# Rotary embedding of attention heads 1 to 3: from GpSimd to VectorE

## The chip, the core and the metric

The kernel runs on one core of a Trainium2 chip. The metric is the device time of one execution in microseconds. Engines are named as in the profile: PE is TensorE (PEld its weight loads), DVE is VectorE, ACT is ScalarE, POOL is GpSimd, SP is SyncE.

## What is computed

One step of a diffusion backbone with one layer: a modulated norm, an input projection, differential attention with four heads beside a depthwise convolution of 31 taps, gates, an output projection, and a gated MLP. There are 1024 latent tokens and 128 context tokens. The change touches the rotary embedding of queries and keys of the latent tokens:

```python
def apply_rope(x, cos, sin):
    shp = x.shape
    xr = x.reshape(shp[:-1] + (2, 2, QK_DIM // 4))
    x1 = xr[..., 0, :]
    x2 = xr[..., 1, :]
    c = cos[None, :, None, None].astype(x.dtype)
    s = sin[None, :, None, None].astype(x.dtype)
    out = jnp.stack([x1 * c - x2 * s, x1 * s + x2 * c], axis=-2)
    return out.reshape(shp)
...
    if rope is not None:
        q = apply_rope(q, rope[0], rope[1])
        k = apply_rope(k, rope[0], rope[1])
```

All arithmetic is fp32. A matmul is made of three, with each operand split into a high and a low part.

## The kernel before

Activations lie with channels on the 128 partitions and the 1152 tokens along the free axis, in three chunks of 384. The program has a first phase that makes the normalised input and the first projections, a second with the attention, and a third with the merge, the output projection and the MLP. The change is in the second.

**Attention and its fillers.** `attn_head` goes over the query tiles of one head, eight of latent tokens and one of context. For each tile and each of the two score maps TensorE makes scores in PSUM (tile `S`, L786 and L787), VectorE takes their minimum (`mx`, L793), ScalarE the exponential (`e`, L795), and VectorE combines the two maps (L803, L804 and the long one, L806, in this document "the combine"). TensorE transposes the combined tile (`T`, L819), ScalarE and VectorE split it into a high part (`ath`, L822) and a low one (`atl`, L823), and TensorE multiplies by the values (`O`, L834). Between these steps stand matmuls of the input projections that are not needed yet, the fillers (L242, PSUM tile `f`), in the order of `FILL_SEQ`: the queries and keys of heads 1 to 3, convolution inputs `ua2`, `ub2`, `ua3`, `ub3`, and gates.

**The rope.** When a filler has made the queries or keys of a head (`xs`, 128x1152), `proj_unit` puts off eight steps of `rope_stages`, one for each of the next ticks: a shuffle on VectorE into `sw` (L550), four multiplications by tables (L558, on `sw`, `xs`, `sw`, `xs`, 128x1024 each), an add (L562), a split in which ScalarE casts the high part `rh` (L566) and the low part is subtracted in place (L567, 128x1152), and the store to DRAM by DMAs on ScalarE's queue. The engine of the six instructions L558 (four), L562 and L567 is chosen by `op_eng`. Ropes are named by head: q0, k0 are made ahead of the attention, and q1, k1, q2, k2, q3, k3 during the attention of heads 0 to 2.

**The convolution in the background.** `conv_jobs` makes each of 31 taps in two parts: 967 columns on VectorE (L651; the first tap is L648, a multiplication alone), and 200 columns as a product on ScalarE (`tap`, L658) that GpSimd adds (L664). The tiles of a head draw them from a list, at a pace set by `PACE`. GpSimd also makes the low halves of the weights (`wlo`, L187), whose high halves ScalarE casts (L180).

**What sets the order.** The program is handed to a scheduler that plans the instructions of each engine by a cost model and priorities (scores, minima, combines and transposes of the attention have a high one); each engine then runs its instructions in the planned order. `pin` limits how far the plan may move an instruction on VectorE, TensorE and SP. So a change of engine also changes the plan around it.

Of the kernel before, what the change touches and what calls it, by code (L numbers as in the profile page):

```python
# [109 lines left out]
class Kernel:  # L110
# [419 lines left out]
    def rope_stages(self, name, xs, sw_t, hi_t):  # L530

        nc = self.nc
        h = int(name[1:])
        isq = name[0] == "q"
        cst = self.cst
        lat = xs[:, NCTX:T]
        lat3 = lat.rearrange("p (r c) -> p r c", c=GRID_W)
        box = {}

        def row(c0):  # L540
            return cst[:, c0:c0 + 16].rearrange("p (r o) -> p r o", o=1).to_broadcast([128, 16, GRID_W])

        def col(c0):
            return cst[:, c0:c0 + 64].rearrange("p (o c) -> p o c", o=1).to_broadcast([128, 16, GRID_W])

        def s0():
            if not isq:
                nc.scalar.dma_start(out=self.A["nk"][h], in_=xs[:, 0:NCTX])
            box["sw"] = sw_t()
            nc.vector.stream_shuffle(box["sw"][:, 0:NLAT], lat, [(i + 16) % 32 for i in range(32)])  # L550

        def op_eng(i):
            return nc.vector if h == 0 else nc.gpsimd

        def mul(i, tab):
            def f():
                v = lat3 if i % 2 else box["sw"][:, 0:NLAT].rearrange("p (r c) -> p r c", c=GRID_W)
                op_eng(i).tensor_tensor(out=v, in0=v, in1=tab, op=ALU.mult)  # L558
            return f

        def add():
            op_eng(4).tensor_tensor(out=lat, in0=lat, in1=box["sw"][:, 0:NLAT], op=ALU.add)  # L562

        def split():
            hi = box["hi"] = hi_t()
            nc.scalar.copy(hi.bitcast(F32R), xs)  # L566
            op_eng(5).tensor_tensor(out=xs.bitcast(F32R), in0=xs, in1=hi, op=ALU.subtract)  # L567

        def store():
            hi = box["hi"]  # L570
            if isq:
                d = self.A["qscr"][h]
                for src, r0, c, o in ((hi, 0, 0, 0), (xs, 0, 0, 64), (xs, 64, 1, 0), (hi, 64, 1, 64)):
                    nc.scalar.dma_start(out=d[o:o + 64, c, :], in_=src[r0:r0 + 64, :])
            else:
                d = self.A["kscr"][h]
                for c in range(2):
                    for o in (0, 64):
                        nc.scalar.dma_start(out=d[o:o + 64, c, 0:T], in_=hi[64 * c:64 * c + 64, :])
                nc.scalar.dma_start(out=d[:, 2, 0:T], in_=xs)  # L580
            self.stored.add(name)

        return [s0, mul(0, row(C_SA)), mul(1, row(C_CA)), mul(2, col(C_SB)), mul(3, col(C_CB)),
                add, split, store]
# [1335 lines left out]
```

## Time and profile before

| | us |
|---|---|
| median of 3 runs (1790.53 to 1791.32) | 1790.59 |
| the profiled execution | 1790.29 |
| its span, from the first to the last instruction | 1788.3 |
| TensorE busy | 1682.3 |
| VectorE busy | 1177.2 |
| GpSimd busy | 713.3 |

Busy time is that of the whole span; a stretch is read by itself, by asking for the busy time of each engine between two times. In a row of instructions the name left of the arrow is what is written, those on the right are what is read; idle time before an instruction stands in brackets with the one that ended it. Waits are put down to the instruction that came last.

### The profile page before, as it was taken

How to read it: one execution, taken by the hardware profiler on the slowest of the kernel's cores; microseconds unless marked ns; L12 is line 12 of the kernel's file. 1: busy time of each engine (PE TensorE's matmuls, PEld its weight loads, DVE VectorE, ACT ScalarE, POOL GpSimd, SP SyncE). 2: the span in 40 equal slices, each digit the busy share in tenths (PEclk: the TensorE clock that was granted, in tenths of full speed). 3: DMA queues.
4: the chain of work that ended last, by engine and by line, in shares of the span. 5: the costliest groups of instructions: out<-in, count | busy, mean ns of one | idle time of the engine just before them, and what ended most of it. 6: DMA issues, size and time to landing. Idle time of an engine off the chain costs nothing.

```text
span 1788.3 us, 25510 instructions
## 1 busy us (share of the span) xinstructions
PE 1682.3 (94%) x9928; PEld 1644.2 (92%) x9928; DVE 1177.2 (66%) x1594; ACT 751.1 (42%) x1166; POOL 713.3 (40%) x507
## 2 busy tenths in 40 slices
PE   5999989989989999889989899999999999999997
PEld 3889989978989999888989899999999999999997
DVE  5859995699697663587588765766567565333335
ACT  4424444445454554311225744545455456111111
POOL 2545782585673431544243321222222137433311
PEclk8999999999999999999999999999999999999999
DMA  8264323323325433666753364756666567622102
GB/s 312 88 190 137 103 79 104 132 69 118 120 76 182 142 105 114 235 221 205 268 174 106 85 173 114 182 131 162 150 151 150 139 148 224 175 89 101 62 12 106
DMA packets 111087, 251.96 MB, mean 141 GB/s; under 512 B 10964, under 2 KB 61816, under 8 KB 108920
## 3 DMA queue, kind: packets, MB, share of 16 engines
q1 hardware_dynamic: 45264, 120.15, 19.7%
q10 hardware_dynamic: 51592, 79.08, 13.9%
q0 software_dynamic: 14112, 51.12, 13.4%
q8 instruction: 78, 1.28, 0.3%
q14 instruction: 41, 0.34, 0.1%
HBM read 161.55 MB, written 57.30 MB: 122 GB/s over the span
## 4 chain that ended last, share of the span: by engine, by line
PE 52%; DVE 18%; DMA 8%; issue 8%; POOL 5%; ACT 3%; ACTq 1%; POOLq 0%; DVEq 0%; SPq 0%
PE f L242 15%; PE T L242 7%; DVE conv L651 7%; PE S L1499 6%; PE f L1499 6%; PE T L1499 6%; PE O L242 3%; PE O L1499 3%; DVE mx L793 2%; DMA tg<-scr_gscr 2%; PE O L834 2%; DVE e L806 2%; POOL wlo L187 1%; DVE S L1206 1%; DMA hx<-in_ada 1%
## 5 line engine op out<-in xcount | busy, mean ns | idle before, releaser
L187 POOL TENSOR_TENSOR wlo<-raw,whi 128x1024 fp32r<-128x1024 f32 x104 | 270.2, 2599 | 389.0 <-ACT whi L180 370.8
L242 PE MATMUL f<-h1h,whi 128*128 128x384 f32 x680 | 233.4, 345 | 3.9 <-ACT gt L614 3.2
L242 PE MATMUL f<-h1l,whi 128*128 128x384 f32 x680 | 234.5, 345 | 0.0
L180 ACT CAST whi<-raw 128x1024 fp32r<-128x1024 f32 x126 | 132.0, 1048 | 243.7 <-DMA raw<-in_wst 59.4
L242 PE MATMUL f<-h1h,wlo 128*128 128x384 f32 x680 | 232.0, 342 | 0.0
L1491 DVE SCALAR_TENSOR_TENSOR X<-X,vec,X 128x1153 f32<-128x1153 f32 x88 | 139.7, 1593 | 91.6 <-ACT X L1489 91.0
L651 DVE SCALAR_TENSOR_TENSOR conv<-glu,vec,conv 128x967 f32<-128x967 f32 x120 | 199.2, 1660 | 1.1
L664 POOL TENSOR_TENSOR conv<-conv,tap 128x200 f32<-128x200 f32 x120 | 115.5, 962 | 68.3 <-ACT tap L658 65.8
L242 PEld LDWEIGHTS f<-h1h,whi 128*128 128x128 f32 x680 | 130.2, 192 | 5.3 <-ACT gt L614 3.9
L242 PEld LDWEIGHTS f<-h1l,whi 128*128 128x128 f32 x680 | 130.7, 192 | 0.4
L242 PEld LDWEIGHTS f<-h1h,wlo 128*128 128x128 f32 x680 | 130.2, 192 | 0.2
L795 ACT ACTIVATE e<-S,mx 128x1152 f32<-128x1152 f32 (+1 forms) x72 | 81.2, 1128 | 70.2 <-DVE mx L793 58.7
L793 DVE TENSOR_REDUCE mx<-S 128x1 f32<-128x1152 f32 (+1 forms) x72 | 88.6, 1231 | 31.5 <-PE S L787 31.5
L658 ACT ACTIVATE tap<-glu,vec 128x200 f32<-128x200 f32 x120 | 55.5, 462 | 105.6 <-POOL conv L664 89.9
L242 PE MATMUL T<-ff,whi 128*128 128x384 f32 x360 | 92.1, 335 | 1.5 <-ACT hx L1691 1.5
L184 POOL DMA_DIRECT2D wlo<-rawx x40 | 34.4, 860 | 141.6 <-ACT wlo L183 122.9
L242 PE MATMUL f<-ff,whi 128*128 128x384 f32 x340 | 87.0, 335 | 0.5 <-ACT hx L1691 0.5
L786 PE MATMUL S<-K,q 128*128 128x384 f32 (+1 forms) x200 | 69.0, 345 | 13.3 <-ACT e L795 13.3
L823 DVE TENSOR_TENSOR atl<-T,ath 128x512 fp32r<-128x512 f32 (+1 forms) x100 | 52.0, 538 | 30.3 <-ACT ath L822 29.8
L1251 DVE SCALAR_TENSOR_TENSOR hx<-f,g,hx 128x128 f32<-128x128 f32 (+1 forms) x64 | 31.6, 515 | 58.8 <-PE f L242 58.8
L180 ACT CAST whi<-rawx 128x1024 fp32r<-128x1024 f32 x42 | 44.0, 1047 | 62.0 <-PE S L1499 23.7
L1251 DVE SCALAR_TENSOR_TENSOR hx<-T,g,hx 128x256 f32<-128x256 f32 (+1 forms) x66 | 32.3, 511 | 54.7 <-PE T L242 54.3
(438 smaller groups left out, 4961.6 us busy)
## 6 DMA issues: line engine op xcount, KB each, us to landing
raw<-in_wst SPq DMA_DIRECT2D x105, 512.0 KB, 4.2
wlo<-rawx POOLq DMA_DIRECT2D x40, 512.0 KB, 6.0
X<-scr_fscr POOLq DMA_DIRECT2D x20, 576.0 KB, 5.0
scr_fscr<-X SPq DMA_DIRECT2D x22, 512.0 KB, 5.3
wlo<-raw POOLq DMA_DIRECT2D x20, 512.0 KB, 4.8
scr_gscr<-gate ACTq DMA_DIRECT2D x48, 192.0 KB, 2.0
tg<-scr_gscr SPq DMA_DIRECT2D x24, 384.0 KB, 4.2
ada<-in_ada SPq DMA_DIRECT2D x8, 1024.0 KB, 9.9
```

The costliest lines, as they stand in the source:

```text
L180: nc.scalar.copy(hi, raw)
L187: eng.tensor_tensor(out=lo, in0=raw, in1=hi.bitcast(F32), op=ALU.subtract)
L242: nc.tensor.matmul(out, lhsT=a, rhs=b, start=(i == 0), stop=(i == n - 1))
L651: t = nc.vector.scalar_tensor_tensor(out=o, in0=glu[:, j:j + CSPLIT], scalar=w[:, j:j + 1], in1=o, op0=ALU.mult, op1=ALU.add)
L658: nc.scalar.activation(out=p, in_=glu[:, CSPLIT + j:CONVW + j], func=AF.Copy, scale=w[:, j:j + 1])
L664: t = nc.gpsimd.tensor_tensor(out=o, in0=o, in1=p, op=ALU.add)
L786: nc.tensor.matmul(S[:, j, :cw], lhsT=qt[:, c, o:o + 128], rhs=self.K[:, c, ks], start=True, stop=False)
L793: nc.vector.tensor_reduce(out=mx[:, 1:2], in_=src, axis=AX.XY, op=ALU.min)
L795: nc.scalar.activation(out=e[:, :w].rearrange("p (a b) -> p a b", a=nk), in_=src, func=AF.Exp, scale=-1.0, bias=mx[:, 1:2], accum_out=self ...
L1251: nc.vector.scalar_tensor_tensor(out=d, in0=ps[:, o:o + ln], scalar=gate[:, j, c:c + 1], in1=d, op0=ALU.mult, op1=ALU.add)
L1491: nc.vector.scalar_tensor_tensor(out=y[:, :L], in0=u[:, t:t + L], scalar=w[:, t:t + 1], in1=y[:, :L], op0=ALU.mult, op1=ALU.add)
L1499: nc.tensor.matmul(ps[:, :CH], lhsT=a[:, ws], rhs=b[:, k], start=first and k == 0 and i == 0, stop=last and k == 3 and i == 2)
```

## The change

The function that picks the engine for the six rope instructions returns VectorE for every head.

```diff
--- before.py
+++ after.py
@@ -550,7 +550,7 @@
             nc.vector.stream_shuffle(box["sw"][:, 0:NLAT], lat, [(i + 16) % 32 for i in range(32)])
 
         def op_eng(i):
-            return nc.vector if h == 0 else nc.gpsimd
+            return nc.vector
 
         def mul(i, tab):
             def f():
```

The plan moves with it. On VectorE, at q1's rope in the attention of head 0, the order before was (`os_590` is the table of the maps' sums):

```order
L550 STREAM_SHUFFLE sw<-xs 128x1024
L651 SCALAR_TENSOR_TENSOR conv<-glu,vec,conv 128x967
L823 TENSOR_TENSOR atl<-T,ath 128x4x128 x2
L651 SCALAR_TENSOR_TENSOR conv<-glu,vec,conv 128x967
L793 TENSOR_REDUCE mx<-S 128x1
L651 SCALAR_TENSOR_TENSOR conv<-glu,vec,conv 128x967 x2
L803 RECIPROCAL mx<-mx 128x1
L823 TENSOR_TENSOR atl<-T,ath 128x128
L804 TENSOR_SCALAR mx<-mx,os_590,lam 128x1
L806 SCALAR_TENSOR_TENSOR e<-e,mx 128x1152
```

and now, from the same shuffle on:

```order
L550 STREAM_SHUFFLE sw<-xs 128x1024
L651 SCALAR_TENSOR_TENSOR conv<-glu,vec,conv 128x967
L823 TENSOR_TENSOR atl<-T,ath 128x4x128
L558 TENSOR_TENSOR sw<-sw,cst 128x1024
L823 TENSOR_TENSOR atl<-T,ath 128x4x128
L558 TENSOR_TENSOR xs<-xs,cst 128x1024
L651 SCALAR_TENSOR_TENSOR conv<-glu,vec,conv 128x967
L558 TENSOR_TENSOR sw<-sw,cst 128x1024
L793 TENSOR_REDUCE mx<-S 128x1
L558 TENSOR_TENSOR xs<-xs,cst 128x1024
L823 TENSOR_TENSOR atl<-T,ath 128x128
L651 SCALAR_TENSOR_TENSOR conv<-glu,vec,conv 128x967
```

The four multiplications and the add stand between taps, minima and splits of the transposed tile; the split (L567) and the combine (L806) follow 6 and 7 rows further on, one after the other.

On GpSimd the same place read, from the last tap add ahead of the rope:

```order
L664 TENSOR_TENSOR conv<-conv,tap 128x200
L558 TENSOR_TENSOR sw<-sw,cst 128x1024
L558 TENSOR_TENSOR xs<-xs,cst 128x1024
L664 TENSOR_TENSOR conv<-conv,tap 128x200
L558 TENSOR_TENSOR sw<-sw,cst 128x1024
L558 TENSOR_TENSOR xs<-xs,cst 128x1024
L664 TENSOR_TENSOR conv<-conv,tap 128x200
L562 TENSOR_TENSOR xs<-xs,sw 128x1024
L187 TENSOR_TENSOR wlo<-raw,whi 128x1024
L664 TENSOR_TENSOR conv<-conv,tap 128x200
L567 TENSOR_TENSOR xs<-xs,rh 128x1152
```

and now:

```order
L664 TENSOR_TENSOR conv<-conv,tap 128x200 x8
L187 TENSOR_TENSOR wlo<-raw,whi 128x1024
L664 TENSOR_TENSOR conv<-conv,tap 128x200 x8
L187 TENSOR_TENSOR wlo<-raw,whi 128x1024
L664 TENSOR_TENSOR conv<-conv,tap 128x200 x7
L187 TENSOR_TENSOR wlo<-raw,whi 128x1024
L631 MEMSET glu 128x15 x3
L187 TENSOR_TENSOR wlo<-raw,whi 128x1024 x4
L917 TENSOR_TENSOR ors<-oms,cols 128x9
```

The six rope instructions are gone, and tap adds and weight halves follow one another.

On VectorE at the first tile of head 1, with q2's rope, the order before was:

```order
L550 STREAM_SHUFFLE sw<-xs 128x1024
L793 TENSOR_REDUCE mx<-S 128x1
L803 RECIPROCAL mx<-mx 128x1
L804 TENSOR_SCALAR mx<-mx,os_590,lam 128x1
L806 SCALAR_TENSOR_TENSOR e<-e,mx 128x1152
L793 TENSOR_REDUCE mx<-S 128x1
L648 TENSOR_SCALAR conv<-glu,vec 128x967
L823 TENSOR_TENSOR atl<-T,ath 128x4x128 x2
L651 SCALAR_TENSOR_TENSOR conv<-glu,vec,conv 128x967
```

and now:

```order
L550 STREAM_SHUFFLE sw<-xs 128x1024
L558 TENSOR_TENSOR sw<-sw,cst 128x1024
L793 TENSOR_REDUCE mx<-S 128x1
L558 TENSOR_TENSOR xs<-xs,cst 128x1024
L558 TENSOR_TENSOR sw<-sw,cst 128x1024
L558 TENSOR_TENSOR xs<-xs,cst 128x1024
L803 RECIPROCAL mx<-mx 128x1
L793 TENSOR_REDUCE mx<-S 128x1
L648 TENSOR_SCALAR conv<-glu,vec 128x967
L562 TENSOR_TENSOR xs<-xs,sw 128x1024
L804 TENSOR_SCALAR mx<-mx,os_590,lam 128x1
L806 SCALAR_TENSOR_TENSOR e<-e,mx 128x1152
```

Three multiplications, a second minimum, the first tap and the add stand between the first minimum and the combine, which came right behind it.

## Rows read from the trace of the kernel before

**Rows 1.** the page: busy us, share of the span and instructions of each engine.
```profile
PE 1682.3 (94%) x9928; PEld 1644.2 (92%) x9928; DVE 1177.2 (66%) x1594; ACT 751.1 (42%) x1166; POOL 713.3 (40%) x507
```

**Rows 2.** busy time by stretch; columns: stretch, us, engines (instructions), clock, DMA share, GB/s.
```profile
206.00:264.00 58.00, 51.99 (x293) 49.54 (x294) 55.80 (x52) 27.85 (x57) 46.57 (x29) 0.94 0.28 78
264.00:337.00 73.00, 71.21 (x455) 70.26 (x454) 34.51 (x54) 31.58 (x64) 19.75 (x14) 1.00 0.39 125
337.00:441.00 104.00, 95.15 (x571) 90.15 (x569) 99.14 (x96) 52.33 (x104) 79.63 (x50) 0.98 0.30 86
...
470.00:552.00 82.00, 72.72 (x436) 68.95 (x435) 79.52 (x75) 42.05 (x83) 65.06 (x39) 0.98 0.34 96
```

**Rows 3.** the chain of waits from 206 to 552 us, its shares by line.
```profile
by line: DVE conv L651 26.7%; PE f L242 18.0%; DVE mx L793 9.3%; DVE e L806 8.9%; DVE atl L823 5.3%; PE O L834 4.1%; issue 2.7%; POOL conv L664 2.6%; PE T L819 2.3%; PE S L786 2.1%; PE S L787 2.1%; ACT e L795 2.0%; DVE sw L550 1.6%; DVE mx 
```

**Rows 4.** one line: durations in ns min/median/max, first and last start us, forms.
```profile
L558 POOL TENSOR_TENSOR xs<-xs,cst x12: 1900/2880/3132, 221.4 to 527.1; 128x1024 f32<-128x1024 f32 x12
...
L558 DVE TENSOR_TENSOR xs<-xs,cst x2: 1206/1208/1211, 87.0 to 93.7; 128x1024 f32<-128x1024 f32 x2
...
L562 POOL TENSOR_TENSOR xs<-xs,sw x6: 2354/2390/3302, 233.0 to 531.6; 128x1024 f32<-128x1024 f32 x6
...
L567 POOL TENSOR_TENSOR xs<-xs,rh x6: 2655/2902/3576, 240.0 to 535.9; 128x1152 fp32r<-128x1152 f32 x6
...
L567 DVE TENSOR_TENSOR xs<-xs,e x1: 1362/1362/1362, 99.6 to 99.6; 128x1152 fp32r<-128x1152 f32 x1
...
L651 DVE SCALAR_TENSOR_TENSOR conv<-glu,vec,conv x120: 1208/1385/3457, 123.1 to 564.6; 128x967 f32<-128x967 f32 x120
```

**Rows 5.** the time line of VectorE, GpSimd and TensorE at k2's rope.
```profile
398.59 3.51 DVE L806 SCALAR_TENSOR_TENSOR e<-e,mx 128x1152 f32<-128x1152 f32 x1
...
398.53 2.35 POOL L562 TENSOR_TENSOR xs<-xs,sw 128x1024 f32<-128x1024 f32 x1
...
402.15 0.47 PE L819 MATMUL T<-cst,e 128*128 128x128 f32 x1 [2.90 <-DVE e L806]
```

**Rows 6.** busy time in the five rope windows (q1, q2, k2, q3, k3).
```profile
218.60:242.70 24.10, 20.48 (x117) 19.55 (x116) 23.29 (x18) 8.00 (x14) 24.07 (x11) 0.93 0.32 94
...
383.60:406.00 22.40, 18.85 (x112) 17.93 (x111) 22.29 (x17) 9.47 (x19) 22.40 (x12) 0.92 0.21 60
...
518.10:538.60 20.50, 17.98 (x102) 16.84 (x101) 20.43 (x14) 8.79 (x17) 20.02 (x11) 0.92 0.23 72
sum 110.30, PE 97.17 PEld 91.82 DVE 107.24 ACT 48.34 POOL 109.22; mean PE 19.43 PEld 18.36 DVE 21.45 ACT 9.67 POOL 21.84
```

**Rows 7.** the same for five windows with taps and without a rope.
```profile
sum 97.00, PE 88.07 PEld 83.37 DVE 93.09 ACT 57.84 POOL 53.81; mean PE 17.61 PEld 16.67 DVE 18.62 ACT 11.57 POOL 10.76
```

**Rows 8.** the taps on VectorE (L651) alone, in the five rope windows.
```profile
218.60:242.70 24.10, 16.41 (x8) 0.93 0.32 94
...
sum 110.30, DVE 61.18; mean DVE 12.24
```

**Rows 9.** the taps (L651) alone, in the five windows without a rope.
```profile
sum 97.00, DVE 50.39; mean DVE 10.08
```

**Rows 10.** combines (L806): seven in the rope windows, then seven in the others.
```profile
sum 110.30, DVE 17.24; mean DVE 3.45
...
sum 97.00, DVE 10.94; mean DVE 2.19
```

**Rows 11.** busy time in the window of k1's rope.
```profile
259.90:278.00 18.10, 17.53 (x113) 16.71 (x112) 13.20 (x15) 7.00 (x14) 16.06 (x12) 1.00 0.37 116
```

**Rows 12.** who waited for whom, 206 to 552 us: us, times, longest us.
```profile
ACT tap L658 <- POOL conv L664: 52.5, 39, 7.1
...
PE T L819 <- DVE e L806: 6.5, 5, 2.9
...
POOL xs L567 <- ACT rh L566: 3.1, 3, 2.0
```

**Rows 13.** busy time and granted clock right after the wait of rows 5.
```profile
402.00:404.00 2.00, 1.85 (x9) 1.85 (x10) 2.00 (x3) 1.46 (x5) 2.00 (x2) 0.54 0.15 35
```

## The prediction

> **What bounds the kernel now.** The page comes first. TensorE is busy for 94% of the span, VectorE for 66%, GpSimd for 40% [rows 1]. The six ropes in question run between 218 and 539 us, so I cut that part of the program where the conv taps on VectorE begin and end [rows 2]. The reader is to see two kinds of stretch. Where taps run (206 to 264, 337 to 441, 470 to 552), VectorE is busy for 95 to 97% and TensorE for 89 to 92%; between them (264 to 337) VectorE is half idle and TensorE at 98%. So VectorE sets the pace in three stretches, 244 us together, and TensorE everywhere else. The chain of waits from 206 to 552 says the same: its largest pieces are VectorE's taps, minima and combines [rows 3]. Five of the six ropes (q1, q2, k2, q3, k3) lie in those three stretches; only k1, at 260 to 278, lies where TensorE is the bound.
>
> The next view is one line's instructions. A rope operation takes GpSimd 1.90 to 3.13 us, the add 2.35 to 3.30, the split 2.66 to 3.58; head 0's, on VectorE, take 1.21 and, for the split, 1.36. The same tap on VectorE takes 1.21 us or up to 3.46, on the same shape [rows 4]. Why, the time line shows: VectorE's combine of 398.59 starts 0.06 us after GpSimd's add and takes 3.51 us, until 1.2 us after the end of that add, and TensorE stands for 2.90 us behind it [rows 5]. So the two engines take turns. A GpSimd operation that is "off" VectorE is paid on VectorE too, and this is the quantity to weigh.
>
> **What it removes.** I put the five ropes' windows side by side with five windows of the same three stretches that hold taps and no rope. In the rope windows GpSimd is busy for 109.2 of 110.3 us, VectorE for 107.2 and TensorE for 97.2 [rows 6]; in the others it is 53.8, 93.1 and 88.1 of 97.0 [rows 7]. Taps: 31 in the rope windows (8, 5, 7, 5 and 6) take 61.18 us, 38 in the others (6, 6, 12, 9 and 5) take 50.39 [rows 8, 9], which is 1.97 and 1.33 us each. Combines: 7 take 17.24 us against 7 that take 10.94, 2.46 and 1.56 each [rows 10]. If the taps fall to what they are without ropes, 31 x (1.97 - 1.33) = 20 us come back; if they fall to the shortest of them, 31 x (1.97 - 1.21) = 24. Combines add 7 x 0.90 = 6. **Back to VectorE: 26 to 30 us.**
>
> **What it adds.** Six instructions for each rope, 5 x 1.21 + 1.36 = 7.4 us by head 0's rows [rows 4], 37 us for five ropes. If each of them meets the GpSimd work that stays (tap adds, weight halves) as a tap does without ropes, it is 0.12 us more for each of 30, 41 us. The durations overlap the next instruction's by some 0.07 us, by the starts in the time line, which takes off 2. **Onto VectorE: 35 to 39 us.** The difference is +5 to +13 us. VectorE is idle for 3.1 us of the rope windows, and an instruction of a rope waits for hardly anything, so it may fill that: +2 to +13. The GpSimd operations that stay are the same in number, and spread over more VectorE instructions, so I lean to the lower half: **+6 us**.
>
> **The smaller terms.** k1's rope goes to a window where VectorE is busy for 13.2 of 18.1 us and TensorE for 17.5 [rows 11]. The 4.9 us of idle time cover most of 7.4; without that cover it costs 2.5. I take 0, since TensorE leads there; both ends stay in the range. The split now waits on VectorE for ScalarE's cast, in front of the combine, where GpSimd waited for it: 3.1 us in 3 waits [rows 12]. By the order, between the add and the split VectorE has about four instructions, a tap, a minimum or a combine of over 1.2 us among them, and the cast is one instruction of 1.15. So 0, and at most 3. On GpSimd nothing is lost: it issues no DMA in this part, its weight halves and tap adds come earlier, and TensorE's waits there are for VectorE and ScalarE. ScalarE's tap waits 52.5 us in all for GpSimd's tap add, up to 7.1 us at a time, and casts for TensorE queue behind it [rows 12]; those waits shrink. But in these stretches ScalarE has time to spare, 48.3 us busy of 110.3 [rows 6], so I count 0 to -3 and take 0. The rope's stores go out on ScalarE's queue as before, and SP's order is unchanged. The order of TensorE's matmuls moves by some 20 places at most, nothing for the sum: what lies in a stretch stays in it.
>
> The sum is 0 outside the three stretches and +6 inside: 1790.29 us of the profiled execution become 1796.3. The median of the runs shown is 0.3 us higher than that execution, so the prediction is **1796.6 us**. A measurement of this kernel tells 0.2%, 3.6 us, from no change.
>
> **A rule to weigh.** The shortest a rope takes GpSimd, without meeting VectorE, is 4 x 1.90 + 2.35 + 2.66 = 12.6 us [rows 4]; five ropes are 63 us. Of these VectorE lost 26 to 30, because its minima and its splits of transposed scores read PSUM and ran alongside. The Trainium skill (SBUF — State Buffer, "Who interferes with whom") says that a VectorE instruction with two SBUF inputs and a GpSimd one that reads SBUF exclude each other, and whichever issues first holds the shared port to its end. The trace agrees in kind: 2.90 us of TensorE's wait stand behind one such turn [rows 5]. Taken alone the rule would put the return at up to 63 us against 35 and the change would be faster; that is a rival below.
>
> **The rivals.** *The port was the true cost (faster).* VectorE's instructions with two SBUF inputs are most of what it has queued in these stretches, so each of GpSimd's operations would hold it up for nearly all of its own 12.6 us. Then VectorE stops being the bound, and what can be gained is TensorE's idle time: at the 90.8% of the other windows [rows 7], 97.2 us of matmuls need 107.0 and not 110.3, 3.3 us less. In the windows of q1, k2 and k3 the mean granted clock is 0.93, 0.92 and 0.92, between the levels of 2.4 and 1.2 GHz, [rows 6]; in k2's it was 0.54 from 402 to 404 us [rows 13], most of that at the lower level, right after TensorE had stood for 2.90 us [rows 5]. If it never fell, their 57.3 us of matmuls were 7.7% or 4.4 us shorter. Together -7.7, rounded to -7: 1783.6 us. For it: GpSimd is busy for 99% of the rope windows. Against it: the measured excess is half of that. It decides if taps come out at 1.21 us and TensorE's share in rope windows at 91% or more.
>
> *Nothing to measure.* VectorE gives 35 and gets 30 back, 3 us of idle time are filled, and ScalarE's shorter waits are worth 2: 0 us, 1790.6. It needs only the lower end of each bound.
>
> *The ropes in front of the combine (slower by more).* The new order puts rope operations between a minimum and its combine. At q2 three multiplications and the add, 4.8 us by their rows, stand where the combine followed its minimum; at q1 the split stands right ahead of the combine. TensorE's transposes wait for the combine, 6.5 us in 5 waits now [rows 12]. If each of five ropes costs 2 us of TensorE's time beyond the sum, less than half of those 4.8, +10 come on top of +6: 1806.6. It decides if TensorE's waits for the combine rise from 6.5 us to over 12.
>
> That the change does not do what it says can be left out: the order has 36 instructions fewer on GpSimd and as many more on VectorE.
>
> **How the numbers follow.** Chances: the forecast (+3.6 to +13) 0.36; ropes before the combine 0.17; nothing to measure 0.27; the port 0.20. So slower by over 0.2%: 0.53, within 0.27, faster 0.20. The likeliest case of one sign is slower, its own range 1794 to 1804. The range that should hold 8 in 10 runs from 1785, halfway into the port's case, to 1806, which takes in the upper bounds of the terms and half of the combine's case.
>
> **What would show it.** In the profile after: L558, L562 and L567 on VectorE for all heads, 1.2 to 1.4 us each where nothing meets them, and none on GpSimd; taps of 1.2 to 1.4 us and none near 3.4 but beside weight halves; combines at 1.5; VectorE at 97% or more in the three stretches, which last 250 us and not 244; a tail after 620 us that is as long as before. Wrong: taps that stay at 1.97 near ropes (the return is missing), TensorE's share in these stretches over 91% (the port's case), or a difference that arises outside 206 to 552 us.

## The result, and the profile after

| | before | after |
|---|---|---|
| median, us | 1791.13 | 1805.34 |
| ratio, 95% interval | | 1.0080 [1.0069, 1.0091] |
| the profiled execution, us | 1790.29 | 1807.39 |
| its span, us | 1788.3 | 1805.6 |

One of the six runs of the changed kernel took 2366.61 us at a granted clock of 0.65; the median and the ratio are those of the other five.

The change makes the kernel slower by 0.80%, 14.3 us with an interval of 12.4 to 16.3. The forecast was +6 us, 1796.6. On its base of 1790.59 us the measured change ends at 1804.9: inside the range, which ends at 1806, and a little above the forecast's own case, which ends at +13.

The page of the changed kernel: first busy us, share of the span and instructions of each engine [rows 1], then the lines of the tap, of GpSimd's tap add and of the scores. At the end of a line stand the busy time in us, the mean ns of one, and the idle time before it with what ended it.

```profile
PE 1687.1 (93%) x9928; PEld 1650.8 (91%) x9928; DVE 1195.1 (66%) x1630; ACT 752.3 (42%) x1166; POOL 607.0 (34%) x471
...
L651 DVE SCALAR_TENSOR_TENSOR conv<-glu,vec,conv 128x967 f32<-128x967 f32 x120 | 175.3, 1461 | 1.2
...
L664 POOL TENSOR_TENSOR conv<-conv,tap 128x200 f32<-128x200 f32 x120 | 102.8, 857 | 87.8 <-ACT tap L658 86.1
...
L786 PE MATMUL S<-K,q 128*128 128x384 f32 (+1 forms) x200 | 70.7, 354 | 34.2 <-ACT e L795 34.2
```

The same lines of the kernel before:

```profile
L651 DVE SCALAR_TENSOR_TENSOR conv<-glu,vec,conv 128x967 f32<-128x967 f32 x120 | 199.2, 1660 | 1.1
L664 POOL TENSOR_TENSOR conv<-conv,tap 128x200 f32<-128x200 f32 x120 | 115.5, 962 | 68.3 <-ACT tap L658 65.8
...
L786 PE MATMUL S<-K,q 128*128 128x384 f32 (+1 forms) x200 | 69.0, 345 | 13.3 <-ACT e L795 13.3
```

The reader is to see three things. 36 instructions went from GpSimd to VectorE. Taps became shorter, 1660 to 1461 ns. And TensorE's idle time ahead of the scores grew from 13.3 to 34.2 us: it waits for the exponential `e` that empties the score tile.

**Where the time arises.** Both executions can be cut at the same events, the starts of certain combines (L806). The windows of the kernel before; columns as in [rows 2]:

```profile
210.20:260.40 50.20, 44.60 (x257) 42.44 (x257) 48.06 (x45) 25.44 (x51) 40.62 (x26) 0.96 0.28 75
260.40:321.40 61.00, 59.13 (x377) 57.89 (x376) 35.28 (x46) 26.94 (x55) 22.74 (x14) 1.00 0.37 108
321.40:427.60 106.20, 97.35 (x589) 92.64 (x588) 89.18 (x95) 50.70 (x101) 73.30 (x45) 0.98 0.34 104
427.60:555.80 128.20, 117.35 (x715) 112.69 (x714) 108.94 (x116) 63.70 (x130) 82.38 (x55) 0.99 0.35 108
555.80:696.30 140.50, 139.29 (x893) 137.62 (x892) 86.93 (x128) 73.85 (x140) 46.24 (x44) 1.00 0.38 130
```

And of the changed kernel:

```profile
210.30:267.90 57.60, 46.49 (x265) 44.10 (x263) 55.92 (x55) 26.49 (x52) 23.14 (x21) 0.94 0.27 79
267.90:328.30 60.40, 57.56 (x361) 57.03 (x362) 34.66 (x48) 26.53 (x52) 7.38 (x6) 0.97 0.32 96
328.30:441.10 112.80, 98.41 (x586) 95.04 (x586) 94.26 (x107) 53.30 (x104) 43.05 (x37) 0.95 0.31 98
441.10:571.60 130.50, 119.11 (x718) 115.25 (x717) 111.49 (x130) 63.31 (x129) 41.59 (x39) 0.96 0.35 106
571.60:712.30 140.70, 139.91 (x893) 137.68 (x893) 87.42 (x128) 72.54 (x138) 44.51 (x44) 1.00 0.38 129
```

Window by window the length changes by +7.4, -0.6, +6.6, +2.3 and +0.2 us, and VectorE's busy time (third engine) by +7.9, -0.6, +5.1, +2.6 and +0.5. The sums are +15.9 and +15.4. So the added work of VectorE shows in the time nearly us for us. The windows that got longer are those in which taps run: the first, with q1's rope and the beginning of k1's, the third, with q2 and k2, and the fourth, with q3 and k3. From 571.6 us on the lateness stays at 16 us to the last combine, and what follows takes 1.3 us more than before (1093.3 and 1092.0).

**What VectorE got back and what it took on.** Groups by line on VectorE from 206 us to just before the 33rd combine, which is 660 us before and 676 after. First the kernel before:

```profile
L651 DVE SCALAR_TENSOR_TENSOR conv<-glu,vec,conv 128x967 f32<-128x967 f32 x80 | 137.1, 1714 | 0.4
...
L806 DVE SCALAR_TENSOR_TENSOR e<-e,mx 128x1152 f32<-128x1152 f32 (+1 forms) x32 | 52.4, 1637 | 0.9
```

and the changed kernel:

```profile
L651 DVE SCALAR_TENSOR_TENSOR conv<-glu,vec,conv 128x967 f32<-128x967 f32 x80 | 113.2, 1415 | 0.4
...
L806 DVE SCALAR_TENSOR_TENSOR e<-e,mx 128x1152 f32<-128x1152 f32 (+1 forms) x32 | 48.6, 1520 | 0.6
...
L558 DVE TENSOR_TENSOR sw<-sw,cst 128x1024 f32<-128x1024 f32 x12 | 16.1, 1345 | 0.0
L558 DVE TENSOR_TENSOR xs<-xs,cst 128x1024 f32<-128x1024 f32 x12 | 15.4, 1287 | 0.0
L562 DVE TENSOR_TENSOR xs<-xs,sw 128x1024 f32<-128x1024 f32 x6 | 10.0, 1664 | 0.0
...
L567 DVE TENSOR_TENSOR xs<-xs,rh 128x1152 fp32r<-128x1152 f32 x6 | 8.3, 1381 | 0.0
```

Taps give back 23.9 us and combines 3.8, 27.7 together. The rope takes 16.1 + 15.4 + 10.0 + 8.3 = 49.8 us for 36 instructions, 1.38 us each.

**How TensorE is held up.** TensorE's groups over the attention, from 206 us to the last combine, with the idle time ahead of them. Before:

```profile
L786 PE MATMUL S<-K,q 128*128 128x384 f32 (+1 forms) x194 | 66.9, 345 | 13.3 <-ACT e L795 13.3
...
L819 PE MATMUL T<-cst,e 128*128 128x128 f32 x291 | 46.5, 284 | 12.7 <-DVE e L806 6.5 <-DVE atl L823 6.1
```

After:

```profile
L786 PE MATMUL S<-K,q 128*128 128x384 f32 (+1 forms) x194 | 68.6, 354 | 33.0 <-ACT e L795 33.0
...
L819 PE MATMUL T<-cst,e 128*128 128x128 f32 x291 | 47.9, 287 | 6.8 <-DVE atl L823 6.3 <-DVE e L806 0.5
```

The wait for the combine has all but gone (6.5 to 0.5 us), and the wait for the score tile took its place, with 19.7 us more. One such wait, at q1's rope, in the time line of the changed kernel (GpSimd's weight half, VectorE, then the exponential and the scores):

```profile
229.84 2.53 POOL L187 TENSOR_TENSOR wlo<-raw,whi 128x1024 fp32r<-128x1024 f32 x1 [2.12 <-ACT whi L180]
...
230.06 3.40 DVE L562 TENSOR_TENSOR xs<-xs,sw 128x1024 f32<-128x1024 f32 x1
233.38 0.15 DVE L803 RECIPROCAL mx<-mx 128x1 f32<-128x1 f32 x1
233.45 1.42 DVE L651 SCALAR_TENSOR_TENSOR conv<-glu,vec,conv 128x967 f32<-128x967 f32 x1
234.80 0.26 DVE L804 TENSOR_SCALAR mx<-mx,os,lam 128x1 f32<-128x1 f32 x1
234.98 1.34 DVE L793 TENSOR_REDUCE mx<-S 128x1 f32<-128x1152 f32 x1
...
236.36 1.22 ACT L795 ACTIVATE e<-S,mx 128x1152 f32<-128x1152 f32 x1 [1.72 <-DVE mx L793]
...
237.72 0.69 PE L786 MATMUL S<-K,q 128*128 128x384 f32 x1 [6.13 <-ACT e L795]
```

The last score matmul of the tile starts at 229.86, so the scores were complete soon after 230.2. Their minimum (L793) starts only at 234.98: the rope's add, which met a weight half and took 3.40 us, a tap and two small instructions stood ahead of it. The next scores write the same PSUM tile, so TensorE runs out of fillers at 231.6 and stands for 6.13 us. Waits of this kind, longer than before's longest of 2.6, begin at 266.2 (3.21), 350.8 (6.25), 419.3 (3.53) and 543.0 us (2.79), in or next to ropes.

### The profile page after: what moved, and what is told of

It is laid out like the page before. It is cut to its first block, busy times and chain, and to the rows that moved or that the text cites. A ratio compares the mean times of both kernels' runs of the same rounds, so it can differ in the third digit from the quotient of the medians.

```text
span 1805.6 us, 25517 instructions
## 1 busy us (share of the span) xinstructions
PE 1687.1 (93%) x9928; PEld 1650.8 (91%) x9928; DVE 1195.1 (66%) x1630; ACT 752.3 (42%) x1166; POOL 607.0 (34%) x471
## 3 DMA queue, kind: packets, MB, share of 16 engines
q1 hardware_dynamic: 45264, 120.15, 19.7%
q10 hardware_dynamic: 51592, 79.08, 13.7%
q0 software_dynamic: 14112, 51.12, 13.3%
## 4 chain that ended last, share of the span: by engine, by line
PE 50%; DVE 6%; DMA 6%; issue 5%; POOL 2%; ACT 1%; ACTq 0%; POOLq 0%; DVEq 0%; SPq 0%
PE f L242 12%; PE T L242 8%; PE S L1499 7%; PE T L1499 7%; PE f L1499 7%; PE O L242 3%; PE O L1499 3%; DMA tg<-scr_gscr 2%; DVE S L1206 1%; PE O L834 1%; DMA hx<-in_ada 1%; DVE conv L651 1%; DMA wlo<-rawx 1%; POOL wlo L187 1%; POOL ml L1157 1%
## 5 line engine op out<-in xcount | busy, mean ns | idle before, releaser
L651 DVE SCALAR_TENSOR_TENSOR conv<-glu,vec,conv 128x967 f32<-128x967 f32 x120 | 175.3, 1461 | 1.2
L664 POOL TENSOR_TENSOR conv<-conv,tap 128x200 f32<-128x200 f32 x120 | 102.8, 857 | 87.8 <-ACT tap L658 86.1
L793 DVE TENSOR_REDUCE mx<-S 128x1 f32<-128x1152 f32 (+1 forms) x72 | 88.7, 1232 | 38.6 <-PE S L787 38.6
L786 PE MATMUL S<-K,q 128*128 128x384 f32 (+1 forms) x200 | 70.7, 354 | 34.2 <-ACT e L795 34.2
L786 PEld LDWEIGHTS S<-K,q 128*128 128x128 f32 x200 | 38.4, 192 | 39.8 <-ACT e L795 39.7
L822 ACT CAST ath<-T 128x512 fp32r<-128x512 f32 (+1 forms) x100 | 45.5, 473 | 60.0 <-PE T L819 55.9
```

The costliest lines, as they stand in the source:

```text
L651: t = nc.vector.scalar_tensor_tensor(out=o, in0=glu[:, j:j + CSPLIT], scalar=w[:, j:j + 1], in1=o, op0=ALU.mult, op1=ALU.add)
L664: t = nc.gpsimd.tensor_tensor(out=o, in0=o, in1=p, op=ALU.add)
L786: nc.tensor.matmul(S[:, j, :cw], lhsT=qt[:, c, o:o + 128], rhs=self.K[:, c, ks], start=True, stop=False)
L793: nc.vector.tensor_reduce(out=mx[:, 1:2], in_=src, axis=AX.XY, op=ALU.min)
```

## The experiments

Two readings were open. In the first, the time is VectorE's sum: each us that the rope adds there lengthens the attention by about one. In the second, the order that the plan made is to blame: the minimum comes late for a score tile that has one buffer, and TensorE stands and then runs at the lower clock.

### The rope left out on either engine, and doubled

In two kernels the four multiplications and the add of heads 1 to 3 are left out, 30 instructions, so queries and keys of these heads are not rotated; one has the split on GpSimd as before, the other on VectorE as after. The third is the changed kernel with each of the 24 multiplications of heads 1 to 3 done twice, which changes the queries and keys of these heads.

```diff
-                op_eng(i).tensor_tensor(out=v, in0=v, in1=tab, op=ALU.mult)
+                if h == 0:
+                    op_eng(i).tensor_tensor(out=v, in0=v, in1=tab, op=ALU.mult)
...
-            op_eng(4).tensor_tensor(out=lat, in0=lat, in1=box["sw"][:, 0:NLAT], op=ALU.add)
+            if h == 0:
+                op_eng(4).tensor_tensor(out=lat, in0=lat, in1=box["sw"][:, 0:NLAT], op=ALU.add)
```

```diff
-                op_eng(i).tensor_tensor(out=v, in0=v, in1=tab, op=ALU.mult)
+                for _ in range(1 if h == 0 else 2):
+                    op_eng(i).tensor_tensor(out=v, in0=v, in1=tab, op=ALU.mult)
```

Left out, split on GpSimd:

> The kernel before, with the four multiplications and the add of heads 1 to 3 left out (the keys and queries of these heads are not rotated); the split stays on GpSimd. Theory A (VectorE's sum: what lies on VectorE in the tap stretches is the time, at about 0.8 us per us): five of the six GpSimd instructions no longer hold the port, some 20 of the 29 us that the change gave back come back, so 12 to 18 us less than the kernel before. Theory B (TensorE's waits: VectorE's work costs only where a score group waits for the one score buffer, and the clock falls behind such a wait): only the stalls near ropes go, 4 to 8 us less.

Left out, split on VectorE:

> The changed kernel, with the four multiplications and the add of heads 1 to 3 left out; the split stays on VectorE. Thirty instructions of some 41 us less on VectorE than the changed kernel has. Theory A: 25 to 32 us less than the changed kernel, so 10 to 16 us less than the kernel before, the same as the run without them on GpSimd. Theory B: 4 to 8 us less than the kernel before.

Doubled:

> The changed kernel, with each multiplication of heads 1 to 3 made twice (the result is not the rotation): 24 more instructions on VectorE, some 30 us. Theory A: 20 to 28 us more than the changed kernel, 36 to 44 more than before. Theory B: the loss comes in lumps where the plan leaves few fillers between two score groups; anywhere from 10 to 50 us more than the changed kernel, and the time at the lower clock grows with it.

| kernel | median, us | ratio to before | attention, us | VectorE busy, us | the rest |
|---|---|---|---|---|---|
| before, in the runs of these three | 1790.19 | 1 | 490.3 | 372.6 | 117.7 |
| after | 1805.34 | 1.0080 [1.0069, 1.0091] | 506.3 | 388.0 | 118.3 |
| left out, split on GpSimd | 1776.22 | 0.9925 [0.9906, 0.9944] | 476.5 | 349.1 | 127.4 |
| left out, split on VectorE | 1772.64 | 0.9907 [0.9889, 0.9925] | 474.4 | 351.6 | 122.8 |
| multiplications twice | 1834.34 | 1.0241 [1.0216, 1.0266] | 529.2 | 411.4 | 117.8 |

"Attention" is the window from 206 us to the last combine in the profiled execution, and "the rest" its length less VectorE's busy time. Each ratio, here and below, is to the kernel before in the same series of runs. The rows of that window of the changed kernel:

```profile
206.00:712.30 506.30, 465.36 (x2837) 452.98 (x2838) 388.02 (x467) 244.21 (x480) 162.02 (x149) 0.97 0.33 106
```

with the rope left out and the split on VectorE:

```profile
206.00:680.40 474.40, 452.69 (x2837) 441.06 (x2838) 351.62 (x437) 242.81 (x480) 162.75 (x150) 1.00 0.35 113
```

and doubled:

```profile
206.00:735.20 529.20, 469.36 (x2814) 455.82 (x2815) 411.36 (x489) 243.87 (x477) 167.52 (x149) 0.95 0.32 101
```

From before to after to doubled, the length less VectorE's busy time stays at 118 us, while VectorE's sum goes up by 39. Idle time of VectorE does not take the added work in. The doubled kernel by itself does not decide between the readings: its 28.8 us more than the changed one lie just above what the first expected and inside what the second did, and the time at the lower clock grew as the second had it (30.7 to 54.6 us). (Of its 45.2 us against before, 6.3 lie behind the attention, for a reason that was not sought.)

The kernels without the rotation speak for the first reading. It expected 12 to 18 and 10 to 16 us less than before, the second 4 to 8; measured are 13.4 [10.0, 16.8] and 16.6 [13.4, 19.9]. In them VectorE's sum falls further than the length (by 23.5 and 21.0 us against 13.8 and 15.9; the rest rises to 127 and 123), so the rule of one us for one us holds for work that is added, and not for all that is taken away. That TensorE then leads for more of the time is the likely reason; it was not tested.

The prices follow. On GpSimd the 30 instructions cost 0.75% of the time, 13.4 us or 0.45 us each [0.33, 0.56]. On VectorE they cost 1.73%, 31 us or 1.03 each [0.91, 1.16], and the 24 more of the doubled kernel 28.8 us, 1.2 each. A multiplication or add of the rope on GpSimd, at 1.90 to 3.30 us of its own [rows 4], is less than half as dear as the same on VectorE. The two kernels without a rotation differ by 0.18%, within their intervals: the split's engine, and the new wait of the split for the cast, cost nothing that can be measured.

### The plan changed, the work kept

The offset that puts the attention's chain ahead in the plan, raised in the changed kernel.

```diff
-HP = 150
+HP = 220
```

> The changed kernel with the priority offset of the attention's instructions at 220 and not 150: the same instructions on the same engines, another plan. Theory A: within 3 us of the changed kernel, since VectorE's sum is the same. Theory B: the loss depends on the plan, 5 us or more away from the changed kernel, to either side.

1802.23 us, ratio 1.0069 [1.0048, 1.0091]: 2 us less than the changed kernel by the ratios, within the intervals, as theory A had it. Its premise held only in part: VectorE's sum is not the same but 6 us lower, since its adds are shorter (1352 ns in the mean and not 1664) and so are its combines (1409 and not 1523). The attention lasts 502.0 us and VectorE is busy for 382.0, again 120 less. TensorE's groups in the attention of this kernel:

```profile
L786 PE MATMUL S<-K,q 128*128 128x384 f32 (+1 forms) x194 | 67.7, 349 | 24.2 <-ACT e L795 24.0
...
L819 PE MATMUL T<-cst,e 128*128 128x128 f32 x291 | 45.6, 279 | 15.9 <-DVE atl L823 8.6 <-DVE e L806 7.1
```

Its wait for the score tile is 9.0 us shorter than in the changed kernel, and that for the transposes 9.1 us longer. In all TensorE stands for 41.7 us, and for 40.9 in the changed kernel. So this plan moved TensorE's waits, and the cost stayed. It is one other plan; that none is better was not shown.

### One rope, and two, on VectorE

The kernel before with k1's rope alone on VectorE, and with q1's and k1's:

```diff
-            return nc.vector if h == 0 else nc.gpsimd
+            return nc.vector if h == 0 or name == 'k1' else nc.gpsimd
```

```diff
-            return nc.vector if h == 0 else nc.gpsimd
+            return nc.vector if h < 2 else nc.gpsimd
```

> The kernel before, with the rope of k1 alone moved to VectorE; it runs in and behind the end of the first tap stretch, where VectorE had 4.9 of 18.1 us idle. Theory A (VectorE's sum in the tap stretches): 0 to 2 us more than before, since most of its 8 us fall into idle time. If each rope costs a sixth of the change wherever it lies: 2.5 us more.

> The kernel before, with the ropes of head 1 (q1 and k1) on VectorE, those of heads 2 and 3 on GpSimd. In the changed kernel's trace the combines are 7 us late after q1 and no later after k1. Theory A: 4 to 7 us more than before, nearly all of it q1's.

k1 alone: 1795.14 us, 1.0031 [1.0022, 1.0040], +5.5 us. Both: 1797.79, 1.0041 [1.0025, 1.0056], +7.3 us. The expectation for k1 was a miss. For both the sum came just above its 4 to 7 us, but not the share: if the costs add, most of it is k1's and not q1's. VectorE's time line of the kernel with k1 alone shows where its rope lies:

```profile
259.74 1.21 DVE L558 TENSOR_TENSOR sw<-sw,cst 128x1024 f32<-128x1024 f32 x1
260.87 1.56 DVE L558 TENSOR_TENSOR xs<-xs,cst 128x1024 f32<-128x1024 f32 x1
262.35 0.15 DVE L803 RECIPROCAL mx<-mx 128x1 f32<-128x1 f32 x1
262.42 1.48 DVE L558 TENSOR_TENSOR sw<-sw,cst 128x1024 f32<-128x1024 f32 x1
263.83 1.34 DVE L793 TENSOR_REDUCE mx<-S 128x1 f32<-128x1152 f32 x1
...
266.73 1.22 DVE L651 SCALAR_TENSOR_TENSOR conv<-glu,vec,conv 128x967 f32<-128x967 f32 x1
```

Three multiplications stand ahead of the minimum of 263.83, and a tap still follows at 266.73, so VectorE's queue was not empty yet. TensorE's next scores start at 266.57, after 3.63 us of idle time that the exponential ended. Its granted clock from 266.5 to 270.0 us is 0.50. VectorE's idle slots in the window [rows 11] lay behind these instructions, not beside them. How the 5.5 us divide between that wait, the clock and VectorE's sum was not separated; in the profile the attention is 8.9 us longer than before and what follows 4.5 us shorter.

### Fewer columns of a tap on VectorE

56 columns of each tap go from VectorE to ScalarE and GpSimd, 256 columns there and not 200; once in the changed kernel, once in the kernel before.

```diff
-CSPLIT = 967
+CSPLIT = 911
```

In the changed kernel:

> The changed kernel, with the taps cut at column 911 and not 967: 56 columns of each tap go from VectorE to ScalarE and GpSimd, whose time the change has made free. 1.04 ns a column by the tap's row, 58 ns for each of some 80 taps, 4.7 us less on VectorE. Theory A: 3 to 5 us less than the changed kernel, 10 to 12 more than before. If the loss is that of the plan alone: no change to speak of.

In the kernel before:

> The kernel before with the same cut at 911. GpSimd is busy there for 99% of the rope windows, and a column costs it about 2 to 3 times what it costs VectorE, which VectorE loses again at the port. Theory A: VectorE gains 4.7 us and loses as much or more, 0 to 5 us more than before.

1807.01 us, 1.0094 [1.0080, 1.0109], in the changed kernel, which is no change from it within the intervals, and 1806.33, 1.0083 [1.0068, 1.0099], in the kernel before. Both were misses. VectorE's groups over the attention, in the kernel before with 911 columns:

```profile
L651 DVE SCALAR_TENSOR_TENSOR conv<-glu,vec,conv 128x911 f32<-128x911 f32 x81 | 138.3, 1707 | 0.5
...
L806 DVE SCALAR_TENSOR_TENSOR e<-e,mx 128x1152 f32<-128x1152 f32 (+1 forms) x35 | 63.7, 1820 | 1.0
```

A tap takes 1707 ns where it took 1714 with 56 columns more, and the combine went from 1637 to 1820. In the changed kernel with 911 columns GpSimd's tap add is longer:

```profile
L664 POOL TENSOR_TENSOR conv<-conv,tap 128x256 f32<-128x256 f32 x84 | 80.3, 955 | 80.0 <-ACT tap L658 76.4 <-PE f L242 2.2 <-DMA qz<-scr_qscr 1.3
```

So VectorE's sum fell by 1.7 us there (388.0 to 386.3) and not by the 4.7 that were worked out for 80 taps. In the kernel before, VectorE's sum rose by 10 us to 382.5. As I read it, what VectorE gives away comes back as time in which it meets GpSimd. That is not all of it: the attention grew by more than VectorE's sum, to 505.9 us in the kernel before and 508.6 in the changed one, 5.7 and 4.0 us beyond it. ScalarE's products are longer too (512 ns and not 462) and the plan is another; these causes were not told apart.

### Ropes moved to stretches without taps

The order of the fillers changed, with ropes on GpSimd as before and then on VectorE. First k1 behind one more gate, with its rope on GpSimd or on VectorE:

```diff
-FILL_SEQ = 'q1 g0 k1 g1 ua2 ub2 q2 g2 k2 g3 ua3 ub3 q3 g4 k3 g5 g6 g7 g8 g9 g10 g11'
+FILL_SEQ = 'q1 g0 g1 k1 ua2 ub2 q2 g2 k2 g3 ua3 ub3 q3 g4 k3 g5 g6 g7 g8 g9 g10 g11'
```

> The kernel before, with the fillers k1 and g1 exchanged: k1's rope, on GpSimd, falls some 20 us later, behind the last tap of the first stretch. Theory A: the last taps of that stretch no longer meet it at the port, 1 to 3 us less than before.

> The same exchange with k1's rope on VectorE, in a stretch in which TensorE leads and VectorE runs no taps. Theory A: 0 to 1.5 us more than the run with it on GpSimd, where k1's rope at its old place cost 5.5 us. If a rope on VectorE costs by the instructions it puts between minima and combines, wherever it lies: 4 to 6 us more.

Then `ua3` and `ub3` behind `k3` as well, so that no taps run in the stretch of q3 and k3, with all ropes of heads 1 to 3 on GpSimd or on VectorE:

```diff
-FILL_SEQ = 'q1 g0 k1 g1 ua2 ub2 q2 g2 k2 g3 ua3 ub3 q3 g4 k3 g5 g6 g7 g8 g9 g10 g11'
+FILL_SEQ = 'q1 g0 g1 k1 ua2 ub2 q2 g2 k2 g3 q3 g4 k3 ua3 ub3 g5 g6 g7 g8 g9 g10 g11'
```

> The kernel before, with the fillers k1 behind g1 and q3, g4, k3 ahead of ua3, ub3: the ropes of k1, q3 and k3, on GpSimd, fall between tap stretches, and the last stretch begins later. Theory A: five of six ropes cost 14 us together by the run without them, so three of them 5 to 7; 3 to 7 us less than before, if the later taps find room in the last stretch, where VectorE is at 64%.

> The same order of fillers with all ropes on VectorE. Theory A: only q1's, q2's and k2's ropes are in tap stretches, 5 to 9 us more than the run with the same order on GpSimd, where the change cost 15. If the place does not matter: 13 to 17 us more.

| order | ropes on | median, us | ratio to before |
|---|---|---|---|
| k1 later | GpSimd | 1802.89 | 1.0057 [1.0039, 1.0076] |
| k1 later | k1's on VectorE | 1799.08 | 1.0041 [1.0029, 1.0054] |
| k1, ua3, ub3 later | GpSimd | 1822.45 | 1.0166 [1.0139, 1.0193] |
| k1, ua3, ub3 later | VectorE | 1826.73 | 1.0187 [1.0162, 1.0212] |

The orders themselves were meant to gain 1 to 3 and 3 to 7 us and cost 10 and 30, which was a miss; the cause was not settled. In the second order two new waits show, 2.79 us at 615 ahead of a transpose of the attention's norm (L923) and 3.6 us ahead of the conv's layer norm (L704), and the lower level of TensorE's clock, 1.2 GHz, for 51 us of the attention (13.7 before).

Within an order the pair compares the engines alone. With k1 in a stretch without taps the rope on VectorE is not dearer than on GpSimd (-0.16%, 2.9 us with some 4 us of uncertainty); the 4 to 6 us more of a cost that does not depend on the place lie outside. The time line of VectorE in that kernel shows idle time behind the add, so there was room:

```profile
290.61 1.22 DVE L562 TENSOR_TENSOR xs<-xs,sw 128x1024 f32<-128x1024 f32 x1
291.74 1.28 DVE L823 TENSOR_TENSOR atl<-T,ath 128x512 fp32r<-128x512 f32 x2
293.60 1.36 DVE L567 TENSOR_TENSOR xs<-xs,rh 128x1152 fp32r<-128x1152 f32 x1 [0.58 <-ACT rh L566]
```

With k1, k3 and most of q3 in such stretches the change of engine costs +0.21%, 3.8 us with some 7 us of uncertainty to either side, against 14.3 in the order of before; 5 to 9 were expected, and 13 to 17 if the place did not matter. Both pairs agree with a cost that hangs on the place and arises where taps keep VectorE full. They do not show it by themselves: the orders cost 10 and 30 us for reasons that stay open, and in the second pair's profiles the attention is even shorter with the ropes on VectorE, 503.0 us against 509.3. No version with the whole computation beats the kernel before.

## Why the prediction was right, and where its size was off

**The direction and its reason hold.** The forecast was slower, because VectorE sets the pace where taps run and takes on more than the port gives back. The windows show lengths that follow VectorE's busy time, and the kernels without and with a doubled rotation show the instructions on VectorE as the cause. The difference lies inside the attention and the end is within 1.3 us of before, as the prediction asked. That the range held is in part luck: its top, 1806, took in half of the combine's case, which did not come, and the bounds of the forecast's own terms end at +13, under the +14.3 measured, though within the interval of the measurement.

**Back to VectorE, 26 to 30 us: right.** 27.7 us were measured, 23.9 of taps and 3.8 of combines (6 were forecast). Some 2.9 of them belong to k1's rope, which the forecast left out: beside it, before, a combine at 260.43 us took 2.63 and a tap at 262.98 took 2.87. The median tap is 1.23 us. Between 206 and 700 us seven taps take more than 2 us, and each stands beside a weight half, as that of 258.42, 3.19 us, beside one of 2.38 on GpSimd at 258.20. The rule of the Trainium skill (SBUF — State Buffer, "Who interferes with whom"), an exclusive turn at a shared port, agrees in kind with this and with the add of 3.40 us at 230.06. Taken alone, for all 63 us of the ropes, it gives too much: they gave back less than half.

**Onto VectorE, 35 to 39 us for five ropes: a little too low.** k1's six instructions lasted 7.45 us (five of 1.22 and one of 1.35), which leaves 42.3 for the others, 1.41 each, where 1.24 was the base and 1.36 the upper bound. The rope instructions now meet weight halves and tap adds themselves: one add met a weight half and took 3.40 us, and nine of the other multiplications and adds took 1.39 to 1.73 beside GpSimd's work. I priced that contention by what taps lose where no rope runs, 0.12 us; it was 0.17. Head 0's ropes, on VectorE in the kernel before, had shown it, in lines that [rows 4] leaves out (durations in ns, min/median/max):

```profile
L558 DVE TENSOR_TENSOR e<-e,cst x2: 1214/2228/3242, 82.6 to 88.1; 128x1024 f32<-128x1024 f32 x2
...
L558 DVE TENSOR_TENSOR ath<-ath,cst x2: 1209/2314/3418, 90.4 to 96.0; 128x1024 f32<-128x1024 f32 x2
```

The two long ones, of eight, stand over weight halves on GpSimd. So 1.21 us was the price of an undisturbed one.

**The step that failed is "so I lean to the lower half: +6 us", with its two supports.** With the overlaps taken off, as the prediction did (0.08 us for each of 30), five ropes are 39.9 us, and 39.9 - 27.7 = 12.2, at the top of +5 to +13 and twice the +6. Without what k1's rope gave back it is nearer to 15. One support was that VectorE's 3.1 us of idle time would be filled. It was not: the attention holds 117.7 us without VectorE before and 118.3 after. More than half of VectorE's idle time up to 676 us is waits for scores (36.7 us) and for the cast of the transposed tile (25.0), inside the chain that runs through VectorE itself; before, up to 660, they were 29.5 and 22.6. When VectorE makes that chain longer, these waits move along with it; so I read it, and the constant 118 us of the doubled kernel agrees. The other was that the tap adds that stay would spread out; they lengthened the rope's instructions as said above.

The rest of the miss is k1's rope, taken at 0: it puts 7.45 us on VectorE and gives some 2.9 back. With these and the first tap (L648: 2.9 to 1.6) the durations add up to +20.9 us. More of VectorE's instructions now follow one another without a pause, and the overlap of neighbours grows from 19.8 to 25.3 us in the attention, which brings it to the +15.5 us of VectorE's busy time; the time follows that.

**k1 at 0: wrong.** By itself it costs 5.5 us, above the bound of 2.5. Its window holds idle time, but its multiplications come at the start, with taps still to run and a minimum behind them. In a stretch that is free of taps from its start the same rope cost no more than on GpSimd, as far as the pair with k1 later shows it.

**"The order of TensorE's matmuls: nothing for the sum": right for the sum, wrong for what shows.** TensorE stands for 12.2 us more (490.30 - 461.59 = 28.7 before, 506.30 - 465.36 = 40.9 after) and is busy for 3.8 more, the 16.0 us once again, seen from the other side. The score tile is where VectorE's lateness reaches TensorE.

**The rivals.** *The port* fell: most taps reached their short length, but the time went up and TensorE is busy for 81% of the first window (46.49 of 57.60 us), not 91%. (Its -7.7 us should have been rounded to -8, 1782.6; nothing hangs on that.) *Nothing to measure* fell: more was taken on than returned. *Ropes in front of the combine* gives nearly the measured time, 1806.6, by the wrong mechanism: its test was the wait for the combine above 12 us, and that is 0.5. The rope stands in front of the minimum, and the wait is for the score tile.

**ScalarE's shorter waits** came as said, 52.5 to 43.3 us for the tap add; no gain from them shows in the time.

## What to carry to other kernels

Where VectorE and GpSimd share the work, price an instruction by what each place takes from VectorE: here 1.03 us on VectorE itself, and 0.45 us for the same instruction on GpSimd, though GpSimd takes 1.6 to 2.6 times as long for a multiplication. Do not let an engine's idle slots pay for added work when these slots are waits inside the chain that the same engine lengthens. And when work put between a PSUM tile's write and its reader makes TensorE stand, do not take that wait for the whole cost: the other plan tried here cut it by 9.0 us, and TensorE stood elsewhere instead.

## What had not been expected of the hardware

**GpSimd's share of a tap is not free for VectorE.** 56 columns moved from VectorE to ScalarE and GpSimd saved nothing and cost 14.9 us in the kernel before: VectorE's taps kept their length (1714 and 1707 ns) and the combine grew by 0.18 us, which is part of the cost; the rest stays open. The Trainium skill (GPSIMD Engine Reference, "4.1 Engine selection") gives elementwise adds and products to VectorE, with GpSimd about half as fast for two inputs. The shortest multiplications here agree with the direction, 1.90 against 1.21 us [rows 4], and the adds with the factor, 2.35 [rows 4] against 1.21. The rope says the opposite for the time: followed here, the advice costs 0.80%.

**TensorE's clock after a wait.** These are the windows of the changed kernel before and after TensorE's return at 237.72, and the same for its return at 357.06:

```profile
231.00:238.00 7.00, 0.87 (x5) 0.55 (x4) 7.00 (x7) 2.79 (x4) 2.85 (x2) 0.88 0.58 171
238.00:245.00 7.00, 7.00 (x30) 6.90 (x31) 7.00 (x8) 3.95 (x9) 2.89 (x4) 0.64 0.45 114
350.00:356.00 6.00, 0.80 (x5) 0.48 (x3) 5.96 (x8) 1.58 (x4) 4.20 (x5) 0.98 0.02 5
356.00:363.00 7.00, 5.94 (x20) 5.94 (x21) 2.52 (x5) 4.98 (x9) 2.84 (x5) 0.53 0.33 93
```

TensorE is busy again, and the granted clock (third column from the right) is 0.64 and 0.53 of 2.4 GHz, most of it at the level of 1.2. Summed over the attention by the clock's records, the lower level holds for 13.7 us before, 30.7 after, 54.6 with the multiplications doubled, and with the rope left out 6.8 (split on GpSimd) and none (split on VectorE). The 3.8 us by which TensorE's busy time grew contain what this costs it directly. What it costs through scores that come later, and so through VectorE's chain, was not measured by itself.
